# Weight splits with priority, small matmuls in a chain, modulation in blocks of 512 columns

## The chip, the core and the metric

The kernel runs on one NeuronCore of a Trainium2 chip. A NeuronCore has five engines, each with its own in-order instruction stream: TensorE (PE) for matrix products, VectorE (DVE), ScalarE (ACT), GpSimd (POOL) and SyncE (SP), which here only issues DMA transfers. Operands live in SBUF, products of TensorE land in PSUM, and the weights come from HBM by DMA. The metric is the device time of one launch in microseconds, as the median of the runs shown; a smaller time is better.

## The reference

The kernel computes one inference step of a one-layer decoder trunk for a prompt (512 tokens) and 8 sample sequences of one token, with a model width of 1024. Cut to what matters here:

```python
mod = silu(c) @ w_mod + b_mod                    # c: 1 prompt row + 8 sample rows; w_mod: 1024 x 6144
sh1, sc1, g1, sh2, sc2, g2 = split(mod, 6)       # "parts" 0..5, 1024 columns each
h = rmsnorm(x) * (1 + sc1) + sh1
u = h @ w_in                                     # 1024 x 8192: q, f, i, og, xb, yb, ga, gb
o_a = rmsnorm(hgrn2(silu(q), k(f), i, logf(f))) * silu(og)      # 8 heads, chunked recurrence
o_b = rglru(conv(xb)) * gelu(yb)                                # 8 blocks
merged = sigmoid(ga) * (o_a @ w_branch_a) + sigmoid(gb) * (o_b @ w_branch_b)
x = x + g1 * (merged @ w_out)
h2 = rmsnorm(x) * (1 + sc2) + sh2
x = x + g2 * (relu(h2 @ w_ff1) ** 2 @ w_ff2)
y = rmsnorm(x)
```

## The kernel before, in words

**Tiling.** Activations stand transposed, features on the 128 partitions and the 520 tokens (512 and 8) along the free axis, in two halves of 260. Every large product runs in three passes: weight and activation are each split into a rounded high part and a remainder low part, and `products` (L107) issues high x high, high x low and low x high. One weight tile is 1024 rows by 128 columns (8 blocks of 128 x 128), so one call of `gemm` (L118) is 8 x 3 x 2 = 48 matmuls. `_split_w` (L70) makes the two parts: ACT casts the staged tile to the high part `whi` (L76), and DVE subtracts it to get the low part `wlo` (L79). `take_w` (L88) hands out the split weights; when it is called for one tile it first issues the splits of the next two (`AHEAD`), and the loads of the next three (`LOADS`) on SP's queue into four staging buffers `wst`. Two pairs of buffers hold the split tiles, so the split of a tile waits until the `gemm` two before it is done.

**Stages.** First, the start: the parts 0 and 1 of the modulation in eight blocks of 256 columns, the normalisation of x and its transposes. Then eight heads (`head`, L479), each with four `gemm`s for its own columns and two more for the RG-LRU branch (`rg_x`, `rg_y`); after each odd head's third `gemm`, `rg_scans` (L736) does exponentials, square roots and a scan on ACT and DVE. Then 32 large products: gates, branch A, and gates and branch B in turn. Then the output projection, and at last the MLP, whose splits go by a plan of their own (`ahead`, L1002) and not through `take_w`.

**A head's small matmuls.** `head_prompt` (L532) builds the products within a chunk from "levels": `level(b)` (L555) makes two DVE operations (L560, L564) and a decay (L567). Two runs of matmuls of 32 output rows follow, all through `small` (L572, matmuls on L573): a first one behind `level(2)`, and a second behind `level(32)` and the sample states (`head_sample`, L516, eight DVE operations on L520). The second run writes two PSUM tiles from the two-buffer pool `pps`: `p` with the blocks of the levels 8, 16 and 32, and `p2` with level 64's and the eight sample products. ACT copies `p2` out (L622, L624), DVE merges `p` under masks (L596, L619). After that the keys are transposed into the one-buffer pool `ppt` (tile `pt`, L633), which the rest of the head uses one after the other (L639, L650, L666, L528).

**Modulation.** Parts 2 to 5 are 32 blocks of 128 columns. `mod` (L345) takes the raw weight tile through `take_w` (the mark `WHOLE` says that it is not split) and issues eight matmuls on L354: the moving operand is the fp32 weight tile, the stationary one 32 columns of the conditioning; the four row groups of the output lie on PSUM partitions 0, 32, 64 and 96. ACT copies the result out (L356); `mod_close` (L362), called behind the last product of the next `gemm`, transposes it (L370), and DVE sums the groups (L374) and adds bias and gain (L378). In `run` (L1345) a step with one block stands behind every large product from the first gate on, until all 32 are placed.

**What sets the order.** Instructions of different engines are ordered by semaphores that a planner writes. The planner simulates a timeline while it places instructions: of those that are ready on an engine it takes the one that comes first in the program, unless a block `high_priority(offset)` moves it so many instructions ahead (`urgent`, L146, uses 200). `behind` (L131) adds an order between two instructions without a semaphore. The order of each engine's stream is then fixed, and the chip waits where an operand is late.

Of the kernel before, what the change touches and what calls it, by code (L numbers as in the profile page):

```python
# [6 lines left out]
F32 = mybir.dt.float32  # L7
# [4 lines left out]
OP = mybir.AluOpType  # L12
# [3 lines left out]
D = 1024  # L16
# [4 lines left out]
KO = D // 128  # L21
H = 8
C = 128
NC = L // C
DFF = 4 * D
EPS = 1e-6
AHEAD = 2
TAIL = 3
URGENT = 200
NWM = 8  # L30
WST = 4
LOADS = 3
MODK = 7
LEAD = 4
WHOLE = "whole"


NM = 9
# [11 lines left out]
class Kernel:  # L50
# [37 lines left out]
    def take_w(self, key):  # L88
        n = self.wcur
        assert self.wspecs[n] == key, (n, self.wspecs[n], key)  # L90
        last = n
        for _ in range(AHEAD):
            last += 1
            while last < len(self.wspecs) and self.wspecs[last][3:] == (WHOLE,):
                last += 1
        while self.wnext_split < min(last + 1, len(self.wspecs)):
            while self.wnext_load < min(self.wnext_split + LOADS, len(self.wspecs)):
                self.wstage[self.wnext_load] = self._load_w(self.wspecs[self.wnext_load], self.wst)
                self.wnext_load += 1
            st = self.wstage.pop(self.wnext_split)  # L100
            spec = self.wspecs[self.wnext_split]
            self.wsplit[self.wnext_split] = st if WHOLE in spec else self._split_w(st, self.split_place())
            self.wnext_split += 1
        self.wcur += 1
        return self.wsplit.pop(n)
# [236 lines left out]
    def mod_key(self, part, k):  # L342
        return (self.i["w_mod"][0], 0, part * D + k * 128, WHOLE)

    def mod(self, keys, w=None):  # L345


        nc = self.nc
        w = w or self.take_w(self.mod_key(*keys[0]))
        n = 128 * len(keys)  # L350
        ps = self.pps.tile([128, 512], F32, name="ps")
        for k in range(KO):
            r = 32 * (k % 4)
            nc.tensor.matmul(ps[r:r + 32, :n], self.cT[:, k, :], w[:, k, :], start=k < 4, stop=k >= KO - 4)  # L354
        ev = self.sm.tile([128, 256], F32, name="modev")
        first = nc.scalar.copy(ev[:, :n], ps[:, :n])  # L356
        self.mod_open = ev, keys
        if self.ppt_free:
            self.mod_close()
        return first  # L360

    def mod_close(self, after=None):  # L362
        nc = self.nc
        ev, keys = self.mod_open
        self.mod_open = None
        n = 128 * len(keys)
        pool, name = (self.ppt, "pt") if self.ppt_free else (self.pps, "ps")
        pt = pool.tile([128, 512], F32, name=name)
        for j in range(len(keys)):
            ins = nc.tensor.transpose(pt[:, j * 128:(j + 1) * 128], ev[:, j * 128:(j + 1) * 128], self.ident)  # L370
            if after:
                self.behind(ins, after)
        s = self.sm.tile([128, 2, NM], F32, name="mods")
        nc.vector.tensor_reduce(s[:, :len(keys)], pt[:, :n].rearrange("p (k j b) -> p k b j", j=4, b=32)[:, :, :NM],  # L374
                                mybir.AxisListType.X, OP.add)
        for j, (part, k) in enumerate(keys):
            g = (self.n1g if part == 1 else self.n2g)[:, k:k + 1] if part in (1, 4) else None
            nc.vector.tensor_scalar(self.modc(part, k), s[:, j], self.bmod[:, part * 8 + k:part * 8 + k + 1], g,  # L378
                                    OP.add, *([OP.mult] if g is not None else []))

    def modc(self, part, k):
        return self.modT[:, part * 8 + k, :]
# [149 lines left out]
    def head_prompt(self, h, f, X, q, v, og, st, vb, fkq):  # L532
        nc = self.nc
# [12 lines left out]
        at = self.at  # L546
# [6 lines left out]
        levels, decay = [X], [f[:, :L], 0]  # L553
# [16 lines left out]
            return made  # L570

        def small(after, *args):  # L572
            ins = nc.tensor.matmul(*args, start=True, stop=True)  # L573
            for x in after:
                self.behind(ins, x)

        def blocks(after, p, c0, x):
            for c in range(NC):
                for j in range(4):
                    s = slice(c * C + 32 * j, c * C + 32 * j + 32)  # L580
                    small(after, p[32 * j:32 * j + 32, c0 + c * 32:c0 + c * 32 + 32], x[:, 1, s], x[:, 0, s])
            return p[:, c0:c0 + 128].rearrange("p (c t) -> p c t", c=NC)

        level(1)
        made = [level(2)]
# [37 lines left out]
        ev = self.hg.tile([128, 256], F32, name="sev", bufs=1)  # L623
# [13 lines left out]
        for c in range(NC):  # L637
            s = slice(c * C, (c + 1) * C)
# [9 lines left out]
        for c in range(NC):  # L648
            s = slice(c * C, (c + 1) * C)
# [5 lines left out]
        for c in range(NC):  # L655
            s = slice(c * C, (c + 1) * C)
# [688 lines left out]
    def run(self):  # L1345
        tc, i, enter = self.tc, self.i, self.ctx.enter_context
# [33 lines left out]
        self.rg = {}  # L1380
# [31 lines left out]
        keys = [k for st in steps for k in st[0]]  # L1412
# [13 lines left out]
    def begin(self):  # L1426

        nc = self.nc
# [5 lines left out]
        raw = {}  # L1434

        def load_mod(n):
            raw[n] = self.start.tile([128, KO, 256], F32, name="wm", bufs=NWM)
            w, r, c, _ = self.mod_key(*mk[n][0])
            nc.sync.dma_start(raw[n], w[r:r + 1024, c:c + 256].rearrange("(k p) n -> p k n", p=128))  # L1439

        def first_w(j):
            st = self._load_w(self.head_cols(0)[j], self.wst)
# [18 lines left out]
        par = self.parameters()  # L1461
        self.decays()
        self.parameters_mod_in(pm)
        evac = self.mod(mk[0], raw.pop(0))
        with self.tc.issue_after(evac.ins):
            self.scale_x()
        x = [self.transposed(k) for k in range(3)]
        for k in range(1, LEAD):
            self.mod(mk[k], raw.pop(k))
# [5 lines left out]
        acc = [self.pmm.tile([128, 2, 512], F32, name="mm") for _ in range(2)]  # L1475
        for k in range(KO):
            if k + LEAD < KO:
                evac = self.mod(mk[k + LEAD], raw.pop(k + LEAD))
# [25 lines left out]
    def begin_tail(self):  # L1504
        self.close_pool()
        tc = self.tc
        self.misc = self.ctx.enter_context(tc.tile_pool(name="misc", bufs=1, side="right"))
        self.right = ExitStack()
        self.abb = self.right.enter_context(tc.tile_pool(name="abb", bufs=16, side="right"))
        self.tail = self.open_pool("tail", 2)  # L1510
        self.ab = self.scope.enter_context(tc.tile_pool(name="ab", bufs=16))
        self.load_branches()

    def begin_strassen(self):
        self.right.close()
        self.sw = self.ctx.enter_context(self.tc.tile_pool(name="sw", bufs=2, side="right", reuse_waits="tile"))


# [32 lines left out]
```

## Time and profile before

| | before |
|---|---|
| runs | 1040.33, 1044.02, 1047.62 us (median 1044.02) |
| the profiled execution, its own time | 1038.48 us |
| its span, from first to last instruction | 1036.3 us |
| PE busy | 992.3 us (96%) |
| DVE busy | 699.7 us (68%) |
| ACT busy | 527.9 us (51%) |
| HBM read | 123.61 MB |

The profile page comes from one execution. Busy time counts an engine as busy while any of its instructions is in flight, so PE's 96% does not say that it worked at its peak; what counts is where its stream stood still, and how much time its pieces take. In a row of the timeline stand start, length, engine, source line, operation, output<-inputs, shapes and how many instructions were merged; in brackets the idle time of that engine just before, with the instruction that ended it. The chain of waits is followed back from the last instruction of a stretch: its pieces are what the end of that stretch hung on, one behind the other. By the stages of the trace: the heads take about 53 to 405 us, the 32 products with the modulation 405 to 617 us, the output projection up to some 680 us, the MLP the rest.

### The profile page before, as it was taken

How to read it: one execution, taken by the hardware profiler on the slowest of the kernel's cores; microseconds unless marked ns; L12 is line 12 of the kernel's file. 1: busy time of each engine (PE TensorE's matmuls, PEld its weight loads, DVE VectorE, ACT ScalarE, POOL GpSimd, SP SyncE). 2: the span in 40 equal slices, each digit the busy share in tenths (PEclk: the TensorE clock that was granted, in tenths of full speed). 3: DMA queues.
4: the chain of work that ended last, by engine and by line, in shares of the span. 5: the costliest groups of instructions: out<-in, count | busy, mean ns of one | idle time of the engine just before them, and what ended most of it. 6: DMA issues, size and time to landing. Idle time of an engine off the chain costs nothing.

```text
span 1036.3 us, 24366 instructions
## 1 busy us (share of the span) xinstructions
PE 992.3 (96%) x10004; PEld 964.7 (93%) x10004; DVE 699.7 (68%) x1583; ACT 527.9 (51%) x1022; POOL 114.1 (11%) x217
## 2 busy tenths in 40 slices
PE   3999999999999999999999999999999999999995
PEld 1799999989989998999999999999999999999995
DVE  6669788686978768564333347667776776777775
ACT  5546654763665365351122234466555655656653
POOL 3200000000000000120000000011422231232040
PEclk9999999999999999999999999999999999999998
DMA  9943344353334334695555578332672474273242
GB/s 302 280 140 109 118 127 140 99 145 114 110 113 127 114 95 147 196 284 147 163 164 163 159 219 213 95 90 61 133 174 82 93 176 121 52 168 88 62 83 83
DMA packets 239472, 143.71 MB, mean 139 GB/s; under 512 B 6526, under 2 KB 234006, under 8 KB 239354
## 3 DMA queue, kind: packets, MB, share of 16 engines
q1 hardware_dynamic: 229458, 130.24, 43.3%
q0 software_dynamic: 9904, 11.92, 6.2%
q8 instruction: 78, 1.28, 0.5%
q14 instruction: 32, 0.26, 0.1%
HBM read 123.61 MB, written 11.26 MB: 130 GB/s over the span
## 4 chain that ended last, share of the span: by engine, by line
PE 85%; DVE 6%; ACT 3%; DMA 2%; SPq 2%; issue 1%; DVEq 0%; ACTq 0%
PE mm L113 61%; PE ps L1091 8%; PE pt L1091 4%; PE ps L354 2%; PE pb L1091 2%; PE ps L573 2%; DVE wlo L79 1%; PE pb L708 1%; DMA wm<-in_w_mod_dram 1%; DVE st L520 1%; SPq L1439 1%; PE mm L1091 1%; DMA wst<-in_w_ff_dram 1%; SPq L67 1%; DVE hs L758 1%
## 5 line engine op out<-in xcount | busy, mean ns | idle before, releaser
L113 PE MATMUL mm<-h,whi 128*128 128x260 f32 (+1 forms) x3072 | 511.5, 286 | 2.0 <-ACT X L135 1.2
L113 PEld LDWEIGHTS mm<-h,whi 128*128 128x128 f32 x3072 | 428.0, 189 | 5.8 <-issue 3.2
L113 PE MATMUL mm<-h,wlo 128*128 128x260 f32 (+1 forms) x1536 | 316.6, 285 | 8.6 <-DVE wlo L79 8.6
L76 ACT CAST whi<-wst 128x1024 fp32r<-128x1024 f32 x166 | 173.9, 1050 | 232.0 <-PE mm L113 193.4
L79 DVE TENSOR_TENSOR wlo<-wst,whi 128x1024 fp32r<-128x1024 f32 x166 | 202.8, 1222 | 97.8 <-ACT whi L76 96.9
L113 PEld LDWEIGHTS mm<-h,wlo 128*128 128x128 f32 x1536 | 240.6, 189 | 11.1 <-DVE wlo L79 9.4
L113 PE MATMUL mm<-a,whi 128*128 128x260 f32 x512 | 85.2, 286 | 0.0
L113 PEld LDWEIGHTS mm<-a,whi 128*128 128x128 f32 x512 | 70.7, 188 | 1.4 <-issue 1.4
L113 PE MATMUL mm<-a,wlo 128*128 128x260 f32 x256 | 51.9, 284 | 0.0
L1187 DVE TENSOR_TENSOR f<-f 128x260 f32<-128x260 f32 x64 | 27.3, 427 | 28.9 <-ACT f L1182 28.3
L803 POOL DMA_DIRECT2D t<-oaT_d x8 | 4.3, 551 | 384.9 <-ACT sq L676 378.0
L1179 POOL TENSOR_TENSOR ft<-ft,fsh 128x8 f32<-128x8 f32 x28 | 18.4, 658 | 219.9 <-DVE ft L1173 219.9
L1176 ACT ACTIVATE ft<-ft,fsh 128x512 f32<-128x512 f32 (+2 forms) x36 | 24.0, 676 | 36.0 <-DVE ft L1173 36.0
L113 PE MATMUL mm<-b,whi 128*128 128x260 f32 x256 | 41.8, 285 | 0.0
L113 PEld LDWEIGHTS mm<-a,wlo 128*128 128x128 f32 x256 | 39.4, 188 | 0.2 <-issue 0.2
L113 PEld LDWEIGHTS mm<-b,whi 128*128 128x128 f32 x256 | 35.0, 188 | 1.6 <-issue 1.6
L560 DVE TENSOR_TENSOR Y<-Y,tb 128x512 f32<-128x512 f32 x48 | 33.0, 687 | 0.7 <-ACT Y L562 0.3
L1221 POOL DMA_DIRECT2D ma<-snap x28 | 27.4, 978 | 35.8 <-issue 31.4
L1203 POOL DMA_DIRECT2D ma<-snap x28 | 26.4, 943 | 43.3 <-DMA ma<-snap 26.6
L819 DVE TENSOR_TENSOR t<-mm,t 128x520 f32<-128x520 f32 x8 | 5.6, 700 | 36.7 <-PE ps L370 36.7
L1182 ACT ACTIVATE f<-ft 128x520 f32<-128x520 f32 (+1 forms) x36 | 20.7, 587 | 15.0 <-POOL ft L1180 12.9
L374 DVE TENSOR_REDUCE mods<-ps 128x9 f32<-128x36 f32 x32 | 6.1, 192 | 30.3 <-PE ps L370 30.3
(488 smaller groups left out, 1869.2 us busy)
## 6 DMA issues: line engine op xcount, KB each, us to landing
wst<-in_w_in_dram SPq DMA_DIRECT2D x64, 512.0 KB, 4.5
wst<-in_w_mod_dram SPq DMA_DIRECT2D x32, 512.0 KB, 6.0
wst<-in_w_ff_dram SPq DMA_DIRECT2D x64, 256.0 KB, 4.7
wst<-in_w_ff_dram SPq DMA_DIRECT2D x32, 512.0 KB, 4.0
wm<-in_w_mod_dram SPq DMA_DIRECT2D x8, 1024.0 KB, 11.3
st<-in_state_hgrn_dram SPq DMA_DIRECT2D x8, 512.0 KB, 5.1
vb<-vd SPq DMA_DIRECT2D x8, 512.0 KB, 3.8
out_dram<-st SPq DMA_DIRECT2D x8, 512.0 KB, 3.4
```

The lines of the kernel that those rows point to most:

```text
L76: ins = self.nc.scalar.copy(hi, st)
L79: self.nc.vector.tensor_tensor(lo, st, hi.bitcast(F32), OP.subtract)
L113: self.last_product = self.nc.tensor.matmul(ps[:, s, :c.stop - c.start], x, y[:, c], start=first and n == 0, stop=last and n == 2)
L354: nc.tensor.matmul(ps[r:r + 32, :n], self.cT[:, k, :], w[:, k, :], start=k < 4, stop=k >= KO - 4)
L560: made = nc.vector.tensor_tensor(view(Y, b, 0, 2 * b, n, b), view(X, b, 0, 2 * b, n, b), fac, OP.mult)
L573: ins = nc.tensor.matmul(*args, start=True, stop=True)
L1091: ins = self.nc.tensor.matmul(ps, x[:, w], y[:, f], start=j in (1, 7, 2) and k == 0 and n == 0, stop=k == 3 and n == 2, skip_group_check=True)
L1176: nc.scalar.activation(t[:, :p], t[:, :p], AF.Relu, bias=sh[:, 0:1])
L1182: nc.scalar.activation(f, self.two(self.ft)[:, a:a + n], AF.Square)
L1187: self.nc.vector.tensor_tensor(f[:, n], f[:, a], f[:, b], op)
L1203: nc.gpsimd.dma_start(x[1][:, b], v[:, :n], accum_op=OP.add)
L1221: nc.gpsimd.dma_start(x[t][:, a], s[p], accum_op=OP.add)
```

## The change

- `_split_w` is called in `take_w` under `urgent()`, so that the casts and subtractions of the weights stand 200 instructions further ahead in the planner's order. (The MLP's own splits are not touched.)
- `small` issues its matmuls 500 instructions ahead, and each one is ordered behind the one before it (`after[:] = [ins]`), so a run is a chain in program order. The first run gets this too.
- The second run begins with `p2`'s matmuls (level 64's and the samples'), then come `p`'s. `p2` moves from `pps` to the one-buffer pool `ppt`.
- The parts 2 to 5 of the modulation are eight blocks of 512 columns in place of 32 of 128. They no longer go through `take_w`: each has a load of 2 MB on SP's queue into one buffer of its own (`wmp`), the first one issued in `begin_tail`, each further one right behind the block before it. The blocks stand behind every third large product from the tenth on. Evacuation, sums, bias and gain are done for four columns of 128 at a time.
- The pool `misc` is opened when `wmp` and the branch operands are released, not at the begin of the tail.

```diff
-        last = n
-        for _ in range(AHEAD):
-            last += 1
-            while last < len(self.wspecs) and self.wspecs[last][3:] == (WHOLE,):
-                last += 1
-        while self.wnext_split < min(last + 1, len(self.wspecs)):
+        while self.wnext_split < min(n + AHEAD + 1, len(self.wspecs)):
...
-            spec = self.wspecs[self.wnext_split]
-            self.wsplit[self.wnext_split] = st if WHOLE in spec else self._split_w(st, self.split_place())
+            with self.urgent():
+                self.wsplit[self.wnext_split] = self._split_w(st, self.split_place())
...
+    def load_mod(self, part, k, n, pool, bufs):
+        w = pool.tile([128, KO, n * 128], F32, name="wm", bufs=bufs)
+        c = part * D + k * 128
+        self.nc.sync.dma_start(w, self.i["w_mod"][0][:, c:c + n * 128].rearrange("(k p) n -> p k n", p=128))
+        return w
...
+    def mod_quarter(self, n):
+        part, k0 = MODS[n]
+        w, self.wmod = self.wmod, None
+        self.mod([(part, k0 + j) for j in range(4)], w, self.wmp.tile([128, 512], F32, name="modev", bufs=2))
+        if n + 1 < len(MODS):
+            self.mod_next(n + 1)
+
+    def mod_next(self, n):
+        self.wmod = self.load_mod(*MODS[n], 4, self.wmp, 1)
...
         def small(after, *args):
-            ins = nc.tensor.matmul(*args, start=True, stop=True)
+            with self.tc.high_priority(offset=SESSION):
+                ins = nc.tensor.matmul(*args, start=True, stop=True)
             for x in after:
                 self.behind(ins, x)
+            after[:] = [ins]
...
-        p2 = self.pps.tile([128, 512], F32, name="ps")
-        found = {b: blocks(made, p, c0, levels[n]) for b, c0, n in ((8, 0, 3), (16, 128, 4))}
-        for c in range(NC):
-            for j in (0, 64):
-                s = c * C + j
-                small(made, p[j:j + 32, 256 + c * 32:288 + c * 32], levels[5][:, 1, s:s + 32], levels[5][:, 0, s + 32:s + 64])
+        p2 = self.ppt.tile([128, 512], F32, name="pt")
...
+        found = {b: blocks(made, p, c0, levels[n]) for b, c0, n in ((8, 0, 3), (16, 128, 4))}
+        for c in range(NC):
+            for j in (0, 64):
+                s = c * C + j
+                small(made, p[j:j + 32, 256 + c * 32:288 + c * 32], levels[5][:, 1, s:s + 32], levels[5][:, 0, s + 32:s + 64])
...
-        mods = [(p, k) for p in (2, 4, 3, 5) for k in range(KO)]
-
-        def mod_step(n=1):
-            for _ in range(n):
-                if mods:
-                    p, k = mods.pop(0)
-                    steps.append(([self.mod_key(p, k)], self.mod, [(p, k)]))
+        quarters, places = list(range(len(MODS))), iter(range(4 * KO))
+
+        def mod_step():
+            at = next(places) - MODS_FROM
+            if at >= 0 and at % MODS_STEP == 0 and quarters:
+                steps.append(([], self.mod_quarter, quarters.pop(0)))
```

Here `MODS_FROM` is 9, `MODS_STEP` 3, `SESSION` 500, and `MODS` lists the eight (part, first column block) pairs in the order of the parts 2, 4, 3, 5.

More of the change, by code (lines that the diff above doesn't have):

```diff
@@ L29 @@
 URGENT = 200
+SESSION = 500
 NWM = 8
@@ L34 @@
 LEAD = 4
-WHOLE = "whole"
+MODS = ((2, 0), (2, 4), (4, 0), (4, 4), (3, 0), (3, 4), (5, 0), (5, 4))
+MODS_FROM, MODS_STEP = 9, 3
 NM = 9
@@ L340, in cond, with mod @@
         self.modT = self.consts.tile([128, 48, NM], F32, name="modT")
-    def mod_key(self, part, k):
-        return (self.i["w_mod"][0], 0, part * D + k * 128, WHOLE)
-    def mod(self, keys, w=None):
+    def load_mod(self, part, k, n, pool, bufs):
[3 more added lines that the diff above has]
+        return w
+    def mod(self, keys, w, ev):
         nc = self.nc
-        w = w or self.take_w(self.mod_key(*keys[0]))
         n = 128 * len(keys)
@@ L354, in mod @@
             nc.tensor.matmul(ps[r:r + 32, :n], self.cT[:, k, :], w[:, k, :], start=k < 4, stop=k >= KO - 4)
-        ev = self.sm.tile([128, 256], F32, name="modev")
-        first = nc.scalar.copy(ev[:, :n], ps[:, :n])
+        first = nc.scalar.copy(ev, ps[:, :n])
         self.mod_open = ev, keys
@@ L365, in mod_close @@
         self.mod_open = None
-        n = 128 * len(keys)
+        part, k0, n = *keys[0], len(keys)
         pool, name = (self.ppt, "pt") if self.ppt_free else (self.pps, "ps")
         pt = pool.tile([128, 512], F32, name=name)
-        for j in range(len(keys)):
+        for j in range(n):
             ins = nc.tensor.transpose(pt[:, j * 128:(j + 1) * 128], ev[:, j * 128:(j + 1) * 128], self.ident)
@@ L372, in mod_close @@
                 self.behind(ins, after)
-        s = self.sm.tile([128, 2, NM], F32, name="mods")
-        nc.vector.tensor_reduce(s[:, :len(keys)], pt[:, :n].rearrange("p (k j b) -> p k b j", j=4, b=32)[:, :, :NM],
+        out = self.modT[:, part * 8 + k0:part * 8 + k0 + n]
+        nc.vector.tensor_reduce(out, pt[:, :n * 128].rearrange("p (k j b) -> p k b j", j=4, b=32)[:, :, :NM],
                                 mybir.AxisListType.X, OP.add)
[L376 to L379, printed above, removed]
+        bias = self.bmod[:, part * 8 + k0:part * 8 + k0 + n]
+        nc.vector.tensor_tensor(out, out, bias[:, :, None].to_broadcast([128, n, NM]), OP.add)
+        if part in (1, 4):
+            g = (self.n1g if part == 1 else self.n2g)[:, k0:k0 + n]
+            nc.vector.tensor_tensor(out, out, g[:, :, None].to_broadcast([128, n, NM]), OP.mult)
+    def mod_quarter(self, n):
[6 more added lines that the diff above has]
+        self.wmod = self.load_mod(*MODS[n], 4, self.wmp, 1)
     def modc(self, part, k):
@@ L1436, in load_mod, with mod @@
         def load_mod(n):
-            raw[n] = self.start.tile([128, KO, 256], F32, name="wm", bufs=NWM)
-            w, r, c, _ = self.mod_key(*mk[n][0])
-            nc.sync.dma_start(raw[n], w[r:r + 1024, c:c + 256].rearrange("(k p) n -> p k n", p=128))
+            raw[n] = self.load_mod(*mk[n][0], 2, self.start, NWM)
+        def mod(n):
+            return self.mod(mk[n], raw.pop(n), self.sm.tile([128, 256], F32, name="modev"))
         def first_w(j):
@@ L1463, in begin @@
         self.parameters_mod_in(pm)
-        evac = self.mod(mk[0], raw.pop(0))
+        evac = mod(0)
         with self.tc.issue_after(evac.ins):
@@ L1468, in begin @@
         for k in range(1, LEAD):
-            self.mod(mk[k], raw.pop(k))
+            mod(k)
         hi, lo = (self.act.tile([128, KO, T2], F32R, tag="h", name="h", bufs=2) for _ in range(2))
@@ L1477, in begin @@
             if k + LEAD < KO:
-                evac = self.mod(mk[k + LEAD], raw.pop(k + LEAD))
+                evac = mod(k + LEAD)
             if k + 3 < KO:
@@ L1506, in begin_tail @@
         tc = self.tc
-        self.misc = self.ctx.enter_context(tc.tile_pool(name="misc", bufs=1, side="right"))
         self.right = ExitStack()
+        self.wmp = self.right.enter_context(tc.tile_pool(name="wmp", bufs=1, side="right"))
         self.abb = self.right.enter_context(tc.tile_pool(name="abb", bufs=16, side="right"))
@@ L1512, in begin_tail @@
         self.load_branches()
+        self.mod_next(0)
     def begin_strassen(self):
         self.right.close()
+        self.misc = self.ctx.enter_context(self.tc.tile_pool(name="misc", bufs=1, side="right"))
         self.sw = self.ctx.enter_context(self.tc.tile_pool(name="sw", bufs=2, side="right", reuse_waits="tile"))
```

## The prediction

> **What bounds the kernel now.** I read the page first, then PE's list of waits, then the chain of waits inside one head and inside the modulation, then the timeline at those places.
>
> ```profile
> span 1036.3 us, 24366 instructions
> ...
> PE 85%; DVE 6%; ACT 3%; DMA 2%; SPq 2%; issue 1%; DVEq 0%; ACTq 0%
> ```
>
> PE carries 85% of the chain that ended last. So a change pays in two ways: PE's pieces get shorter, or a wait of PE goes. PE's waits between 53 and 617 us, where everything lies that the change touches, are three:
>
> ```profile
> PE mm L113 <- DVE wlo L79: 8.6, 4, 2.4
> PE ps L573 <- DVE a L596: 1.5, 3, 0.5
> PE mm L113 <- ACT X L135: 1.2, 1, 1.2
> ```
>
> Four times a `gemm` waits for a weight's low part (8.6 us), three times a second run waits for a PSUM buffer that DVE frees (1.5 us). The third is the begin of the first head, which the change leaves alone. The profiled execution took 1038.48 us and the median is 1044.02: I make the sum against 1038.5 and add 5.5 for the forecast.
>
> **Part 1, the modulation in larger blocks.** The first fence is the chain of waits in the middle of the modulation stage, with one row from the heads; its columns are start, length, line and count.
>
> ```profile
> 442.23 0.11 PE ps L370
> 442.34 0.57 PE ps L354 x16
> 442.91 5.97 PE mm L113 x48
> 448.88 0.11 PE ps L370
> ```
>
> ```profile
> 236.39 13.08 PE mm L113 x109
> ```
>
> One round of this stage is 448.88 - 442.23 = 6.65 us and nothing but PE. A product undisturbed takes 13.08/109 = 0.120 us, so 48 take 5.76. The transpose (0.11) stays: 32 of them before and after. What is left, 6.65 - 5.76 - 0.11 = 0.78 us, is the price of one block of 128 columns: its 16 instructions and what the products before and behind lose when PE changes over. 32 of them cost 25.0 us.
>
> For more columns the start has blocks of 256. A row of PE's timeline for each size:
>
> ```profile
> 39.91 1.07 PE L354 MATMUL ps<-wm,cT 128*32 128x256 f32 x16
> ```
>
> ```profile
> 442.27 0.64 PE L354 MATMUL ps<-wst,cT 128*32 128x128 f32 x16
> ```
>
> 128 more columns cost 1.07 - 0.64 = 0.43 us, the count of instructions being the same. Two more steps of that size to 512 make a block 0.78 + 3 x 0.43 = 2.07 us, eight of them 16.6 us. The saving is **25.0 - 16.6 = 8.4 us**. Its bounds: nothing, if a block of 512 costs four of 128; 18.8 us at the other end, if the columns cost nothing and only the changeover did (8 x 0.78 = 6.2); the rows lie on a line that gives 8.4, and I take that.
>
> [...]
>
> What rides along: ACT's copy, the reduction and the bias are fewer instructions on engines that are half idle there (next fence: DVE 72.28 and ACT 51.30 of 177 us), at no cost to PE. The loads move the same 16.8 MB, 2 MB at a time, each behind the previous block's matmuls on SP's queue, and the weight loads queue up behind them. What hides them is three products and a block, 3 x 5.76 + 2.07 + 0.44 = 19.8 us, in which 2.10 + 3 x 0.52 = 3.67 MB must come: 185 GB/s.
>
> ```profile
> 440.00:617.00 177.00, 177.00 (x1742) 167.09 (x1740) 72.28 (x131) 51.30 (x87) 7.67 (x16) 1.00 0.63 183
> ```
>
> The stage (columns: window, length, busy time of PE, PEld, DVE, ACT, POOL, then clock, DMA share, GB/s) moved 183 GB/s at a DMA share of 0.63, so full use would be some 290. The first block stands six products behind the issue of its load. I cost the loads at nothing.
>
> Without eight blocks between the first gates, branch A begins about 8 x 0.89 = 7 us sooner after the heads. Its operands were split by 448.8, its first product stood at 456.15:
>
> ```profile
> 447.37 1.41 DVE L162 TENSOR_TENSOR a<-t,a 128x520 fp32r<-128x520 f32 x2 [1.42 <-ACT a L161]
> ```
>
> ```profile
> 456.15 0.75 PE L113 MATMUL mm<-a,whi 128*128 128x260 f32 x4
> ```
>
> The last operand is used only seven eighths into that `gemm`, 5 us later. Five us of slack remain; cost nothing.
>
> **Part 2, splits with priority.** The wait for `wlo` sits in the odd heads. The chain of waits there, from 116 to 134 us in head 1:
>
> ```profile
> 116.77 1.28 ACT L750
> ...
> 118.73 0.71 DVE gate L756
> ...
> 119.47 1.23 DVE hs L758
> ...
> 122.39 2.09 DVE st L520 x8
> 124.48 1.13 DVE wlo L79
> ...
> 126.67 1.22 DVE hs L758
> ...
> 128.76 1.12 DVE wlo L79
> ...
> 130.03 0.33 DVE Y L564
> 130.35 0.61 DVE y L775
> 130.96 0.22 DVE a L596
> ...
> 131.22 1.08 PE ps L573 x30
> ```
>
> ```profile
> L750 ACT ACT_TABLE_LOAD x4 | 5.1, 1283 | 0.1
> ```
>
> The first piece is a table load, as ACT's row for it in the heads (four of 1283 ns) shows. And PE in the same stretch, the stalled product and the begin of the second run:
>
> ```profile
> 125.67 0.51 PE L113 MATMUL mm<-h,wlo 128*128 128x260 f32 x2 [2.08 <-DVE wlo L79]
> ...
> 129.70 1.01 PE L573 MATMUL ps<-Y 128*32 128x32 f32 x80
> ```
>
> The chain is DVE all the way from 118.73 to 131.18: the ACT load of the square root's table made DVE late, and DVE works without a pause until PE's second run hangs on it. PE's stall at 123.6 is not on this chain. With priority `wlo` goes ahead of the sample states (L520) or of the scan, and the 2.08 us stall goes. But both `wlo` of the chain stand ahead of level 32's copy (L564) already, so that copy still ends at 130.36, and the second run needs it. PE is there 2 us sooner and waits there.
>
> **Part 3, the second run.** It takes 1.81 us when nothing holds it (the next fence: it starts at 221.35, the next product at 223.16). Before, `p`'s part ran while `p2` waited for its buffer. Now `p2` is first, has a buffer in `ppt`, and needs level 32 at once. I work out the end of the run at each place, as level 32's end plus 1.81.
>
> ```profile
> 221.35 1.39 PE L573 MATMUL ps<-Y 128*32 128x32 f32 x94
> ...
> 223.16 0.50 PE L113 MATMUL mm<-h,whi 128*128 128x260 f32 x2
> ```
>
> ```profile
> 220.06 0.42 DVE L564 COPY Y<-Y 128x512 f32<-128x512 f32 x1
> ```
>
> ```profile
> 402.39 0.42 DVE L564 COPY Y<-Y 128x512 f32<-128x512 f32 x1
> ```
>
> ```profile
> 402.31 1.43 PE L573 MATMUL ps<-Y 128*32 128x32 f32 x94
> ```
>
> ```profile
> 353.63 1.01 PE L573 MATMUL ps<-Y 128*32 128x32 f32 x80
> ```
>
> ```profile
> 354.30 0.42 DVE L564 COPY Y<-Y 128x512 f32<-128x512 f32 x1
> ```
>
> Head 1: 130.36 + 1.81 = 132.17, before 131.22 + 1.08 = 132.30, gain 0.1. Head 3: 220.48 + 1.81 = 222.29, before 223.16, gain 0.9. Head 7: 402.81 + 1.81 = 404.62, before 402.31 + 1.81 = 404.12, loss 0.5. Head 6, which has no split stall: 354.72 + 1.81 = 356.53, before 353.63 + 1.81 + 0.5 = 355.94, loss 0.6. Head 5 I take as head 1, the other even heads as even. The heads together: **about 0**. Bounds: the whole 8.6 + 1.5 = 10.1 us won, if the planner puts the run later or DVE gets there sooner; 8 x 0.6 = 4.8 us lost, if every head does as head 6. I take 0, because the chain above is the row nearest to the question.
>
> The bank: `p2` in `ppt` comes behind the previous head's last reader (L530) and ahead of this head's key transposes (L633).
>
> ```profile
> 116.92 0.16 DVE L530 COPY os<-pt 128x8 f32<-128x8 f32 x1
> ```
>
> ```profile
> 133.81 0.36 ACT L624 COPY sev<-ps 128x256 f32<-128x256 f32 x1
> ```
>
> ```profile
> 134.86 0.60 PE L633 MATMUL pt<-ident,Y 128*128 128x128 f32 x4
> ```
>
> In head 1, L530 ends 12.6 us ahead of the run, and ACT's last copy of `p2` ends 134.17, 0.7 us ahead of the transposes. Both are covered; without that cover a head would lose what the copy is late. The chain within a run and its higher priority change nothing that I can see: the run stands in one piece already. The sum: 1038.5 - 8.4 - 0 = 1030.1, as a median **1035.6**; I say 1035.
>
> **The rivals.** *The stalls go.* DVE's backlog is made good because a split placed early fills one of the holes that ACT's table load leaves, or the run is placed behind more products. For: 10.1 us stand in the list of waits, named. Against: the chain. Time: 1038.5 - 8.4 - 10.1 = 1020.0, as a median 1025.5. Chance 0.30.
>
> *The loads become the bound, slower than before.* One buffer per block means that a load starts only when the block before is done. The start's 1 MB blocks took this long to land:
>
> ```profile
> wm<-in_w_mod_dram SPq DMA_DIRECT2D x8, 1024.0 KB, 11.3
> ```
>
> Twice that is 22.6 us against 19.8 hidden: each of seven blocks (the first has a longer lead) is 2.8 us late even with no weight tile between, 20 us in all, 1035.6 + 20 = 1055.6. It decides from 1.2 us late per block (8.4/7), that is under some 175 GB/s. Against: 290 GB/s worked out above, and the 11.3 us were met with all eight loads queued at once. Chance 0.07.
>
> *The blocks do not scale:* a block of 512 costs four of 128, the modulation gains nothing, 1044. [...] Chance 0.10.
>
> **How the numbers follow.** The forecast has a chance of 0.53. Within 1% of before means 1033.6 to 1054.5, about what a measurement of this kernel can tell from no change. Faster: the rival without stalls (0.28 of its 0.30) and that part of the forecast where the heads give 2 us or more (0.15): 0.43. Slower: most of the load rival and a little of the heads' loss, 0.07. The same: 0.50. The range goes from 1024, below the rival without stalls, to 1043, the forecast with the heads' loss of 4.8 and some spread of the runs.
>
> **What would show it.** Part 1: rows of L354 with 128x512, sixteen in about 1.9 us, and rounds without a block of 5.76 us; a wait of L354 for a DMA would be the load rival. Part 2: no wait of L113 for `wlo` L79 between 53 and 405 us. Part 3: in its place waits of L573 for DVE's Y L564 or st L520, near 2 to 3 us in the heads 1, 5 and 7; if the sum of PE's waits in the heads is under 3 us, the forecast is wrong and the rival without stalls is right. A second run far later in PE's stream than level 32's end would say the same.

## The result, and the profile after

The changed kernel took 1032.58 us (median of four runs, 1029.11 to 1032.71), the kernel before 1043.4 (the three runs listed above and a fourth of 1042.78). The ratio is 0.9886, with a 95% interval of 0.9845 to 0.9926: 1.1% faster. The profiled execution took 1032.62 us, its span is 1030.6 us against 1036.3. One later launch of the changed kernel, in the experiment that repeats it, took 1952.14 us at a granted clock of 1.0; its cause is not known, and it is left out of the medians and ratios below.

From the page of the changed kernel: the span, the busy times, and the chain that ended last by engine.

```profile
span 1030.6 us, 23395 instructions
...
PE 985.0 (96%) x9620; PEld 956.8 (93%) x9620; DVE 691.3 (67%) x1533; ACT 524.2 (51%) x998; POOL 112.1 (11%) x217
...
PE 83%; DVE 5%; ACT 3%; DMA 3%; issue 1%; DVEq 0%; ACTq 0%
```

PE carries 83% of the chain where it carried 85%, and ACT's and DMA's shares (3% and 3%, before 3% and 2%) have not gone. So this line gives no sign that PE became freer of waits. PE's waits between 53 and 407 us of the changed kernel (us in total, times, longest) say that it did not:

```profile
PE pb L718 <- ACT xcs L158: 5.6, 3, 1.9
PE mm L110 <- DVE wlo L81: 4.5, 5, 1.3
PE pt L643 <- DVE hlast L771: 2.1, 2, 1.3
PE mm L110 <- ACT X L132: 1.2, 1, 1.2
```

Together 13.4 us, where before 8.6 + 1.5 + 1.2 = 11.3 us stood: PE waits 2.1 us longer in the heads than it did. The wait of the second run is gone (L573, now L582), that for `wlo` is half as long, and in their place stand one of the block-diagonal product (L718) for the cast `xcs` on ACT and one of the key transposes (L643).

The modulation is where the time went. The chain of waits there (start, length, line, count), and PE's timeline at one block:

```profile
464.00 1.85 PE ps L352 x16
465.86 0.54 PE ps L801 x4
...
473.09 5.76 PE mm L110 x48
478.85 0.44 PE ps L367 x4
```

```profile
463.93 1.92 PE L352 MATMUL ps<-wm,cT 128*32 128x512 f32 x16
```

A block of 512 columns takes 1.85 us on the chain, and a round without a block 5.76. (L801 transposes the convolution's last columns, which happen to stand behind this block; L367 are the four transposes of a block.) PE has no wait at all between 407 and 640 us, not for a load either, and from the third on the blocks' loads are issued 19.8 us apart, which is what the prediction gave three products and a block.

Counting the matmuls of `products` in both traces in the order in which they ran, the last of 84 `gemm`s of 48, a little behind the modulation stage, ends at 639.2 us against 645.3, 6.1 us sooner. If the heads lost what their waits say, 2.1 us, the modulation won 6.1 + 2.1 = 8.2 us.

What is new among DVE's waits points to where the heads lost. First before, then after, DVE's wait for the broadcast of the sample values `vb`:

```profile
DVE st L520 <- DMA vb<-vd: 1.7, 2, 1.3
```

```profile
DVE st L528 <- DMA vb<-vd: 16.6, 8, 4.0
```

The eight sample states (L528, L520 before) multiply a row that goes to HBM (`vd`) and comes back to all 128 partitions (`vb`). In the changed kernel they stand earlier in DVE's stream than the row is back, in all eight heads. The chain of waits between 158 and 176 us (head 2, an even one) of the changed kernel:

```profile
157.32 2.39 DMA vd<-vs
...
159.72 4.21 DMA vb<-vd
...
164.23 1.14 DVE st L528 x4
...
165.56 0.79 DVE st L528 x3
...
166.42 1.13 DVE wlo L81
...
171.64 1.12 DVE wlo L81
172.76 0.67 DVE xc L735
...
174.02 0.64 ACT xcs L158
...
174.70 0.39 PE pb L718
```

And of the kernel before in the same window:

```profile
162.44 1.15 PE ps L573 x83
163.59 9.13 PE mm L113 x74
172.72 1.81 PE ps L573 x94
```

The two ends of the changed kernel's chain in the timeline, DVE's and PE's (in brackets the idle time before, and what ended it):

```profile
163.96 1.14 DVE L528 SCALAR_TENSOR_TENSOR st<-vb,fkq,st 128x128 f32<-128x128 f32 x4 [2.69 <-DMA vb<-vd]
```

```profile
174.70 0.39 PE L718 MATMUL pb<-xcs,bdhlru_wa 128*128 128x260 f32 x1 [1.86 <-ACT xcs L158]
```

Before, the chain of this head is PE all the way. After, it runs from a DMA through DVE's work of the head to ACT's cast. DVE works almost without a pause from 163.96 on. So the reading is that the 2.69 us which it lost at its first state operation come out at PE eleven us later, as 1.86; the experiments test it.

### The profile page after: what moved, and what is told of

It is laid out like the page before. It is cut to its first block, busy times and chain, and to the rows that moved or that the text cites. A ratio compares the mean times of both kernels' runs of the same rounds, so it can differ in the third digit from the quotient of the medians.

```text
span 1030.6 us, 23395 instructions
## 1 busy us (share of the span) xinstructions
PE 985.0 (96%) x9620; PEld 956.8 (93%) x9620; DVE 691.3 (67%) x1533; ACT 524.2 (51%) x998; POOL 112.1 (11%) x217
## 4 chain that ended last, share of the span: by engine, by line
PE 83%; DVE 5%; ACT 3%; DMA 3%; issue 1%; DVEq 0%; ACTq 0%
PE mm L110 60%; PE ps L1101 8%; PE pt L1101 4%; PE pb L1101 2%; PE ps L352 1%; DMA vb<-vd 1%; PE pb L718 1%; DVE wlo L81 1%; PE ps L582 1%; DVE st L528 1%; PE mm L1101 1%; DMA vd<-vs 1%; PE pt L660 1%; PE pt L649 1%; DVE xc L735 1%
## 5 line engine op out<-in xcount | busy, mean ns | idle before, releaser
L528 DVE SCALAR_TENSOR_TENSOR st<-vb,fkq,st 128x128 f32<-128x128 f32 x64 | 18.1, 348 | 16.6 <-DMA vb<-vd 16.6
L352 PE MATMUL ps<-wm,cT 128*32 128x256 f32 (+1 forms) x256 | 25.5, 523 | 3.6 <-DVE pl L218 2.1
```

The source lines that it names most:

```text
L528: last = nc.vector.scalar_tensor_tensor(st[:, b], vb[:, b], fkq[:, 1, b:b + 1], st[:, b], OP.mult, OP.add)
```

## The experiments

Four questions: which part of the change carries the time, whether ACT's table loads or the broadcast make DVE late, whether the heads' loss can be had back, and what the splits' priority is worth. Ratios are to the kernel before, run beside each on the same chip, with their 95% intervals; they are estimated from all the runs and need not be the quotient of the two medians shown. The groups of experiments ran on three chips, so kernels of different groups are best compared by their ratios.

**The blocks alone.** The changed kernel with the splits without priority and the second run as it was:

```diff
-            with self.urgent():
-                self.wsplit[self.wnext_split] = self._split_w(st, self.split_place())
+            self.wsplit[self.wnext_split] = self._split_w(st, self.split_place())
...
-            with self.tc.high_priority(offset=SESSION):
-                ins = nc.tensor.matmul(*args, start=True, stop=True)
+            ins = nc.tensor.matmul(*args, start=True, stop=True)
...
-            after[:] = [ins]
...
-        p2 = self.ppt.tile([128, 512], F32, name="pt")
+        p2 = self.pps.tile([128, 512], F32, name="ps")
```

> The modulation in eight blocks alone; splits without priority, the second run as before. Theory (the blocks carry the gain, the heads' waits only move): 8.4 us less than before, about 1035, and the heads' two waits of before (8.6 us for wlo, 1.5 us for the mask merge) still there. Rival (the heads' part pays): at most 2 us more than the kernel after, that is 1034 or less is expected by the theory too, but the kernel with the heads' part alone then has to be 2 us or more faster than before.

Measured: 1032.58 us against 1041.8, ratio 0.9897 (0.9877 to 0.9916). PE's waits in the heads:

```profile
PE mm L109 <- DVE wlo L81: 8.6, 4, 2.4
PE ps L580 <- DVE a L603: 1.4, 4, 0.5
```

They are those of before to 0.1 us, so the blocks leave PE's waits in the heads as they were, and the blocks alone carry as much as the whole change. "The blocks" here are the width, the place in the program, the loads and the pool together; no run takes these apart.

**The heads' parts alone.** The priority, the chain and the bank, with the 32 blocks of 128 columns as before:

```diff
-        quarters, places = list(range(len(MODS))), iter(range(4 * KO))
+        mods = [(p, k) for p in (2, 4, 3, 5) for k in range(KO)]
```

> The heads' part alone: splits with priority, small matmuls chained, p2 first and in the other bank; modulation as before, in 32 blocks. Theory: no gain, 1041 to 1046, PE's waits in the heads about 12 us in all, as in the profile after (xcs, wlo, hlast). Rival: the waits of 10.1 us go, 1033.

Measured: 1044.05 us (12 runs) against 1041.8, ratio 1.0011 (0.9992 to 1.0029). PE's waits, and DVE's for the broadcast:

```profile
PE pb L712 <- ACT xcs L163: 5.6, 3, 1.9
PE mm L115 <- DVE wlo L80: 4.4, 5, 1.6
PE pt L637 <- DVE hlast L765: 1.9, 2, 1.1
```

```profile
DVE st L522 <- DMA vb<-vd: 15.9, 7, 3.6
```

The heads' parts are worth nothing that can be measured, and they bring the new waits with them, whatever the modulation does.

**Blocks and priority, without the run's edits.** As the kernel with the blocks alone, but with the splits under `urgent` as in the change:

```diff
-            with self.tc.high_priority(offset=SESSION):
-                ins = nc.tensor.matmul(*args, start=True, stop=True)
+            ins = nc.tensor.matmul(*args, start=True, stop=True)
...
-            after[:] = [ins]
...
-        p2 = self.ppt.tile([128, 512], F32, name="pt")
+        p2 = self.pps.tile([128, 512], F32, name="ps")
```

> The kernel after with the second run and the small matmuls as before: blocks and splits with priority. Theory: the wait for wlo goes or shrinks and waits for DVE come up elsewhere (second run, key transposes) of about the same sum; 1032 to 1037. Rival: 1043 - 8.4 - 8.6 = 1026.

Measured: 1034.82 us, ratio 0.9911 (0.9882 to 0.9940).

```profile
PE ps L581 <- DVE a L604: 7.9, 5, 2.4
PE mm L110 <- DVE wlo L81: 3.5, 4, 2.5
```

```profile
DVE st L528 <- DMA vb<-vd: 2.8, 3, 1.5
```

Two readings. The priority moves the wait: 8.6 us at `wlo` become 3.5, and 1.4 us at the second run become 7.9. And the wait for `vb` stays small (2.8 us; 3.1 with the blocks alone), so the priority of the splits alone does not put the sample states early. The edits of `small` and of the second run do, alone or together with it.

**The changed kernel again**, beside these three:

> The kernel after once more, beside the others on the same chip. The profile says 6 us less than before, the medians 10.8: theory (blocks 8.4 less, heads and start 2 more): 6 less, 1037. Rival: 10.8 less.

Measured: 1031.08 us (five runs), ratio 0.9894 (0.9865 to 0.9922). By its ratio that is about 11 us less, 8 to 14 by the interval: the rival, and not the theory of 6 us, was borne out. Blocks alone, blocks with priority and the whole change lie within one another's intervals.

**No table loads.** In the scans the exponential, the tanh and the square root become sigmoids; ACT's table loads between 53 and 410 us, 1283 ns each, go from twelve to one by this. The outputs that hang on the scans are then other numbers. First in the kernel before, then in the changed one.

```diff
-            self.grouped(nc.scalar.activation(a, r, AF.Exp, scale=self.c8n[:, n:n + 1]))
-            self.grouped(nc.scalar.activation(r, r, AF.Tanh, scale=self.c8[:, n:n + 1]))
+            self.grouped(nc.scalar.activation(a, r, AF.Sigmoid, scale=self.c8n[:, n:n + 1]))
+            self.grouped(nc.scalar.activation(r, r, AF.Sigmoid, scale=self.c8[:, n:n + 1]))
...
-            root = nc.scalar.activation(u, u, AF.Sqrt)
+            root = nc.scalar.activation(u, u, AF.Sigmoid)
```

> The kernel before with the exponential, the tanh and the square root of the RG-LRU scans put as sigmoids, which are no part of the reference: same sizes and engines, but ACT loads no table between them. Theory (ACT's three table loads per pair of heads, 1.28 us each, make DVE late in the odd heads and PE waits for that): the four waits for wlo go from 8.6 us to under 3, 1043 - 6 = about 1036. Rival (the split is merely placed too late by the planner): the 8.6 us stay.

> The kernel after with the same sigmoids in place of exponential, tanh and square root. Theory: PE's waits in the odd heads (wlo about 3, hlast about 2) go; those of the even heads (xcs 5.6) stay, since they come from the samples' broadcast; 1032 - 4 = about 1028. Rival: no wait changes.

Measured, in the kernel before: 1036.66 us against 1043.39, ratio 0.9947 (0.9919 to 0.9975). Its waits:

```profile
PE ps L573 <- DVE a L596: 3.7, 4, 2.1
PE mm L113 <- DVE wlo L79: 3.5, 2, 2.2
```

In the changed kernel: 1032.07 us, ratio 0.9887 (0.9862 to 0.9911).

```profile
PE pb L718 <- ACT xcs L158: 5.6, 3, 1.9
PE mm L110 <- DVE wlo L81: 3.7, 4, 1.3
```

```profile
DVE st L528 <- DMA vb<-vd: 17.3, 8, 3.5
```

So the kernel before gains without the table loads (10.1 us of waits become 7.2), but less cleanly than expected: the wait for `wlo` fell to 3.5 us and not under 3, that of the second run rose from 1.5 to 3.7, and DVE's wait for `vb` rose from 1.7 to 9.2 us. In head 1 the states stand in the same place as before, but DVE comes to them 1.89 us ahead of the row. So part of what the loads had cost seems to go into that wait; that is not shown by a run of its own. In the changed kernel I had expected some 4 us, and nothing came: the 2.1 us at `hlast` and 0.8 of the 4.5 at `wlo` went, and the 5.6 at `xcs`, behind the wait for `vb`, stayed. Besides, the profiled execution without the table loads had a mean granted clock of 0.988, the changed kernel's 0.994; the last section shows how time and clock went together.

**No way through HBM.** `vb` is filled from a row of the inputs, which is there from the start, in place of `vd`; so the sample states are other numbers. With and without the table loads:

```diff
-        nc.sync.dma_start(vb.rearrange("p b v -> p (b v)"),
-                            vd.rearrange("b v -> (b v)").partition_broadcast(128))
+        nc.sync.dma_start(vb.rearrange("p b v -> p (b v)"), self.i["c_prompt"][0].partition_broadcast(128))
```

> The kernel after, with the samples' values vb broadcast from an input row in place of the row just written to HBM, so that the transfer needs no v of this head (that part of the samples' state is left out). Theory: DVE no longer stands 2.7 us at the sample states in the even heads, and the three waits for xcs (5.6 us) go: about 1027. Rival (xcs is late because the splits go ahead of it): they stay.

> Both at once: no table loads in the scans and no broadcast of this head's values. Theory: PE's waits in the heads fall from about 12 us to under 3, 1032 - 10 = about 1022. Rival: at least half of them stay.

Measured with the table loads: 1022.67 us (two runs), ratio 0.9809 (0.9722 to 0.9896), 8 to 10 us under the changed kernel, by the ratios or by the medians. PE's waits that are left:

```profile
PE pt L581 <- DVE Y L571: 3.1, 3, 1.2
PE mm L110 <- ACT X L132: 1.2, 1, 1.2
PE pt L642 <- DVE Y L571: 0.7, 3, 0.2
PE mm L110 <- DVE wlo L81: 0.5, 1, 0.5
```

5.5 us in place of 13.4. Without the table loads too: 1018.86 us (two runs), ratio 0.9772 (0.9685 to 0.9859), and of PE's waits only the one for `X` is left. So once the wait for `vb` is away the table loads do cost something, 3.8 us by these medians; beside it they were hidden. This points to the broadcast as the cause, with one reserve: the planner, too, reckons with another load here and places the states much earlier (in head 1 they begin at some 90 us, where they began at 119.76). So the run takes away a wait and rearranges DVE's stream at once.

**The sample states late.** A kernel that leaves nothing out: the changed one, with the state operations ordered behind level 32's on DVE, and their eight matmuls last in the second run.

```diff
-    def head_sample(self, h, st, vb, fkq):
+    def head_sample(self, h, st, vb, fkq, after):
...
+            self.behind(last, after)
...
-        state = self.head_sample(h, st, vb, fkq)
         level(16)
-        made = [level(32), state]
+        made = [level(32)]
+        state = self.head_sample(h, st, vb, fkq, made[0])
...
+        made.append(state)
+        for b in range(NB):
+            j, c = 32 * (b % 4), 256 + 128 * (b // 4)
+            small(made, p2[j:j + 32, c:c + 128], fkq[:, 2], st[:, b])
```

> The kernel after, with the sample states' operations held behind level 32 on DVE, and their products put last in the second run. Nothing is left out. Theory (DVE stands still for the broadcast vb, 16.6 us in all, because the planner puts the states where the chip does not have vb yet; the even heads' waits of PE follow from it): DVE's wait for vb falls under 6 us, PE's waits for xcs (5.6 us) go, about 1026. Rival (it is not the place of the states but the splits ahead of xc): xcs stays at 5 us or more, 1032.

Measured: 1019.17 us (1018.81 to 1021.87) against 1042.97, ratio 0.9773 (0.9754 to 0.9793): 12 us under the changed kernel by the ratios, 13 by the medians, and 2.3% under the kernel before. All PE waits of its heads:

```profile
PE mm L110 <- ACT X L132: 1.2, 1, 1.2
PE pt L583 <- DVE Y L573: 1.0, 1, 1.0
PE mm L110 <- DVE wlo L81: 0.4, 1, 0.4
```

2.6 us in place of 13.4, and among DVE's waits that for `vb` is not listed any more. DVE's timeline of an odd head (head 1) shows the order:

```profile
122.21 1.22 DVE L81 TENSOR_TENSOR wlo<-wst,whi 128x1024 fp32r<-128x1024 f32 x1
...
125.68 0.69 DVE L569 TENSOR_TENSOR Y<-Y,tb 128x512 f32<-128x512 f32 x1
...
127.22 0.42 DVE L573 COPY Y<-Y 128x512 f32<-128x512 f32 x1
127.56 0.61 DVE L528 SCALAR_TENSOR_TENSOR st<-vb,fkq,st 128x128 f32<-128x128 f32 x2
```

The states' operations now stand behind level 32's copy, and with them what they would wait for. The copy ends at 127.64; before it ended at 130.36, in the changed kernel at 128.08. What the changed kernel had late in this head is the split: it came behind the states, which began at 119.76 after a wait of 1.05 us:

```profile
123.89 1.23 DVE L81 TENSOR_TENSOR wlo<-wst,whi 128x1024 fp32r<-128x1024 f32 x1
```

Here it starts at 122.21, 1.7 us sooner, of which 0.7 is the earlier start of the first `gemm` (29.3 against 30.0 us).

**The transpose and copy of `vs` sooner.** The other way to close the gap: bring the row earlier, by putting its transpose and its copy under `urgent`. Alone, and together with the late states:

```diff
-        nc.tensor.transpose(ps[:NB, :128], v[:, L:], self.ident)
-        vs = self.hg.tile([NB, 128], F32, name="vs", bufs=1)
-        nc.vector.tensor_copy(vs, ps[:NB, :128])
+        with self.urgent():
+            nc.tensor.transpose(ps[:NB, :128], v[:, L:], self.ident)
+            vs = self.hg.tile([NB, 128], F32, name="vs", bufs=1)
+            nc.vector.tensor_copy(vs, ps[:NB, :128])
```

> The kernel after, with the transpose and the copy of the samples' values moved 200 instructions ahead, so that the write and the broadcast start sooner; the states stay where they are. Theory: the copy on DVE comes up to 2 us sooner, DVE's wait for vb falls from 16.6 us to about 8, PE's waits in the heads by some 3 us, about 1029. Rival: the transpose already follows the product closely, nothing changes, 1032.

> Both edits on the kernel after. Theory: DVE's wait for vb is under 3 us and PE's waits in the heads are those of the odd heads alone, 3 to 5 us; 1024 to 1026. Rival: as the kernel after, 1032.

Measured: 1033.86 us alone, ratio 0.9901 (0.9874 to 0.9928); DVE's wait for the row is what it was:

```profile
DVE st L529 <- DMA vb<-vd: 15.9, 8, 3.2
```

Together with the late states 1020.49 us, ratio 0.9776 (0.9755 to 0.9798), the late states' time. The priority did not bring the row sooner: in head 1 the copy stands 1.90 us behind the transpose with it and without it. Of the two ways tried, only the place of the row's readers helps.

**Late states, splits without priority.** To see what the priority is worth once DVE is in time:

```diff
-            with self.urgent():
-                self.wsplit[self.wnext_split] = self._split_w(st, self.split_place())
+            self.wsplit[self.wnext_split] = self._split_w(st, self.split_place())
```

> The kernel with the late sample states, but the splits without priority, as before. Theory (once the broadcast no longer holds DVE, the priority of the splits is what ends the odd heads' wait for wlo): that wait is back with 5 us or more, 1025 to 1028. Rival (the late states alone give DVE its 2.2 us ahead of the split back, and the priority adds nothing): within 2 us of 1019.

Measured: 1021.71 us against 1043.6, ratio 0.9788 (0.9764 to 0.9813), with the same three waits as the late states with priority, 1.2, 1.0 and 0.4 us. I had expected a loss of 5 us or more; the intervals overlap. The two profiled executions differ by 2.2 us, of which 1.75 lie ahead of the first `gemm`; the mean granted clock was 0.994 in this one and 0.997 in the other. So, with the states late, the odd heads' wait for `wlo` is gone with the priority and without it, and the priority adds nothing that can be measured.

## Why the prediction was right, and where it was not

**The blocks: right in mechanism, and nearly in size.** The forecast was 8.4 us; the trace gives 8.2, the run of the blocks alone 9.2 by its median and 10.7 by its ratio (8.8 to 12.8), so 8.4 is at or a little under the low end. The sixteen instructions of a block of 512 were to take 0.64 + 3 x 0.43 = 1.93 us in the timeline and take 1.92. With its changeover the block was to take 2.07 us; on the chain it takes 1.85, and the four transposes behind it 0.54 where four others take 0.44, so 1.95. Eight of them are 15.6 us, and the saving by these rows would be 25.0 - 15.6 = 9.4. In the trace of the blocks alone the 84th `gemm` ends at 637.8, 7.5 us sooner than before, with a granted clock of 0.98 from 140 to 230 us and again from 230 to 320, where the kernel before has 0.98 and 1.00; with 1.7 us for that, an estimate (0.02 of 90 us is 1.8, and the last section has 1.5 to 1.7), the count gives 9.2. In the trace of the whole change about 1 us less shows, and I have no row for that. The round without a block is 5.76 us, as worked out. No wait for a load was there, which ends the rival of the loads. (Its 11.3 us was not met "with all eight loads queued at once": the eight were issued between 3.6 and 26.8 us.) And 1.92 us against four blocks of 0.64 ends the rival that the blocks don't scale.

**The heads: the sum was right, the mechanism only in part.** Forecast 0, measured 1.0011 (0.9992 to 1.0029) with the heads' parts alone. That a stall of PE moves when the engine behind it is late was shown by the run of blocks and priority: there the wait went to the second run, where Part 2 had put it, with 7.9 us (for the buffer that the merge of `a` frees). In the changed kernel it stands elsewhere. The prediction named as its signs no wait for `wlo` in the heads, and waits of the second run in the heads 1, 5 and 7; the trace has 4.5 us for `wlo` still, 5.6 at L718 in even heads and none at the second run. The step that failed is the sentence of Part 3 that the chain within a run and its higher priority "change nothing that I can see". The run's edits, these two or the new place of `p2`, changed the place of the sample states in DVE's stream, and with it the wait for `vb` went from 1.7 to 16.6 us. The row with 1.7 us was in the list of DVE's waits of before, and it was the sign: states that already wait up to 1.3 us for their operand can't be moved earlier at no cost. That other waits of about the same sum came in place of the old ones is luck, not the working of Part 3.

**The table loads.** Part 2 began its chain with one. Taking them away gave 0.5% in the kernel before, nothing that can be measured in the changed one, and 3.8 us where the wait for `vb` was away.

**The rival without stalls** had its price about right, but not for this change. The late states bring the waits from 11.3 to 2.6 us, 8.7 us where the rival named 10.1; but it takes another order of DVE's work for that, not priority.

**The 5.5 us between profile and median** were added as a constant, and they are none: the changed kernel's profiled execution (1032.62) lies on its median. The sum of the profile, 1030.1, was 2.5 us too low, about the heads' 2.1, and the constant 5.5 too high. That the two errors have opposite signs and leave 1035 only 2.4 above the result is luck. Part of the difference goes with PE's clock, as the last section shows.

**What stays open.** Which of the run's three edits (chain, priority, `p2` first in another bank) makes the planner place the states early was not taken apart. In the run without the way through HBM, wait and order changed together; the late states settle that the order is enough, not how much the way itself costs. They move the states' matmuls in PE's run as well as the operations on DVE, and they were not tried without the run's other edits.

## What to carry to other kernels

Where each block costs the bound engine a fixed price beside its columns (here 0.78 - 0.43 = 0.35 us), fewer and wider blocks win, and the gain can be read off beforehand, as here from two sizes in the trace (8.4 us forecast, 8.2 by the trace). A stall of the bound engine that hangs on an engine without slack can move when priority is given to the one operand, as it did here (8.6 us at `wlo` became 3.5, and 1.4 us at the second run 7.9): follow the chain through the late engine, and ask what its stream holds that nobody needs yet. In a stream that a planner orders, work on a row that goes through HBM and back belongs behind the work that others wait for, by an explicit order (here DVE's wait of 16.6 us for the row left the list, and the kernel took 12 us less by the ratios), and after every edit nearby its wait is to be looked up again.

## What the hardware showed beside this

**PE's granted clock stood at 0.50 for 3.41 us once in each of the traces of before and after, between 50 and 1000 us, and each time behind a wait of PE of 1.86 us or more.** Windows of the changed kernel: length, busy times of PE, PEld, DVE, ACT and POOL, then the granted clock, DMA share, GB/s. The first two are around the wait at L718 in head 2, the other two around the one in head 4.

```profile
172.51:175.92 3.41, 1.55 (x34) 1.44 (x25) 2.81 (x8) 1.65 (x4) 0.00 (x0) 1.00 0.40 108
175.92:179.33 3.41, 3.41 (x19) 3.41 (x18) 3.40 (x12) 1.52 (x3) 0.00 (x0) 0.50 0.75 200
264.67:268.08 3.41, 2.15 (x115) 1.90 (x113) 2.87 (x6) 0.57 (x2) 0.00 (x0) 1.00 0.22 67
268.08:271.49 3.41, 2.81 (x23) 2.81 (x24) 3.35 (x10) 1.52 (x5) 0.00 (x0) 1.00 0.97 265
```

In head 2 PE stood for 1.86 us in front of L718, the granted clock was then 0.50 for 3.41 us, and four products took 1.07 us (at 176.70) in place of 0.65 (at 179.57). What that cost is an estimate: half of 3.41, 1.7 us, by the granted clock, and 1.5 us by the rows, where six products took 1.30 us (176.70 to 178.00) and later 0.72 (182.18 to 182.90). In head 4 PE stood for 1.86 us too, and the clock stayed at 1.00. The windows are cut 3.41 us long from the begin of head 2's slow stretch, and their border splits the wait of head 4 into 1.26 and 0.60 us. In the kernel before the place is in head 3, at 0.50 from 216.22 to 219.63, behind a wait of 2.05 us for `wlo`. With both traces cut that way, each from its own slow stretch, PE was idle for 1.86 us (after) and 2.05 us (before) in the window ahead of it, and for no more than 1.27 and 1.72 us in any other between 50 and 1000 us. So the length of the wait alone does not tell the two waits of 1.86 us apart, and the idle time in the window does. These are two places in two traces; no kernel here was made to test it.

In the late states' trace the clock from 170 to 180 us reads 1.00, where the changed kernel's reads 0.83, and the mean over the span is 0.997 against 0.994. If their heads lose nothing to the clock, the sum closes: 10.8 us fewer waits, the 1.5 to 1.7 us of clock estimated above and a first `gemm` that begins 0.7 us earlier come to 13.0 to 13.2 us, where the spans differ by 13.1 (1030.6 and 1017.5).

The runs' spread goes with the clock as well. In the 45 runs of the kernel before that stood beside the experiments, the mean granted clock lay between 0.987 and 0.995 (median 0.991) and the time between 1046.87 and 1037.76 us; a straight line through them gives 0.7 us for each 0.001 (correlation -0.76). The profiled execution of before, at 0.995 and with its one such place, was among the fastest. That is a correlation over runs, and it does not hold for all: one run of the changed kernel had a mean of 0.946 and took 1032.71 us, as the others did.

**The way of 4 KB through HBM** took 2.39 us out and 4.21 us back to 128 partitions, as the chain of head 2 shows: 6.6 us, and DVE stood 2.69 us for its end.
